# Modulation of a gated two-branch layer computed in three column pieces instead of two

## The chip, the cores and the metric

The kernel runs on one core of a Trainium2 chip. The metric is the device time in microseconds of one execution. Three runs of the kernel before gave 1683.67, 1685.21 and 1689.54 us; the median is 1685.21.

The engines named below: PE (matrix products; PEld is its weight load), DVE (vector), ACT (scalar, activations), POOL (GpSimd) and SP, whose queue issues the DMAs. They run side by side and each executes its instructions strictly in program order, waiting on semaphores for the others.

## The reference

One layer is computed, for 1024 latent tokens and 256 context tokens of 1024 channels, all in fp32. What matters here is its beginning: a modulation vector per stream (latent and context) is a product of a SiLU of the conditioning with `w_ada`; its first 2048 columns are shift and scale for 1024 channels each. The tokens are RMS-normalised, scaled and shifted, and projected by `w_in`.

```python
def rms_norm(t):
    tf = t.astype(jnp.float32)
    return (tf * lax.rsqrt(jnp.mean(tf * tf, axis=-1, keepdims=True) + EPS)).astype(t.dtype)

def modulate(t, shift, scale):
    return rms_norm(t) * (1 + scale) + shift
...
        mod_x = jax.nn.silu(c) @ w_ada[layer] + b_ada[layer]
        mod_c = jax.nn.silu(c_ctx) @ w_ada[layer] + b_ada[layer]
        sh_x, sc_x, g_x = jnp.split(mod_x[:, None, :], 3, axis=-1)
        sh_c, sc_c, g_c = jnp.split(mod_c, 3, axis=-1)
        pl = project(modulate(x, sh_x, sc_x), w_in[layer])
        pc = project(modulate(ctx, sh_c, sc_c), w_in[layer])
```

Behind it come the two branches (gated linear attention, differential attention), their gates and the output projection. They are not touched.

## The kernel before

Tokens come in ten tiles of 128 (0 to 7 latent, 8 and 9 context), channels in eight blocks k of 128. The projection needs each channel block of the modulated tokens with channels on partitions, split into a high and a low fp32r part; one fp32 product then takes three fp32r products (`mm3`, line 340), recorded at line 335.

**How the order is made.** The kernel is written as many generators. A small planner (`Driver`, line 59) runs them against estimated costs and writes PE's, ACT's, DVE's and POOL's instructions in the order in which it would start them. That order is fixed when the kernel is built, and each engine keeps it whatever the data do on the chip. SP's DMAs are placed by the framework's own scheduler; up to eight of them are in flight. Buffers are counted by tag (`acq` and `rel`, lines 316 and 324): `w` has 18 of 128x512, `raw` 3, `l5` 3, `pl` 4, `g5` (token tiles) 6, `tp` (PSUM for transposes) 2.

**The opening** (`prologue`, lines 488 to 661) has these tasks:

- `loads` (515): the weights of the modulation. Its 1024 channels are taken in two halves. For each block k of rows, half 0 loads shift columns and scale columns separately, 128x512 each; among these loads stand the token tiles 0 to 3 (the table `XL`, 663). Then follow the first two weight tiles of the projection (`RAWS`) and the eight loads of half 1, 128x2x512 each. After that the task waits for `ev_wc` (543), which is set when all of half 1 has been split (564), and only then loads the tiles 4 to 9.
- `xnorm` (498): one token tile: ACT squares it with a sum, POOL makes the reciprocal root, DVE scales the tile.
- `conv` (549): splits half 1 of the modulation weights into high (ACT) and low (DVE) parts.
- `ada` (566): the products. Half 0 runs as 16 full fp32 products with two output rows (latent and context): shift into the PSUM tile `gs`, scale into `go`. Half 1 runs as 32 fp32r products of the split weights. The results are copied out of PSUM (`gs` by ACT, `go` by DVE, 590 to 597), transposed by PE into `gt` (4 channels blocks each for shift and scale), and added to the bias by DVE into `shsc`, from which a block's shift and scale are read.
- the main body (647 to 661): for each token half (tiles 0 to 3, 4 to 7, then 8 and 9) and each block k, it waits for `ev_sh[k // 4]`, transposes four token tiles into `tp`, and starts `hblock` (623): ACT applies scale and shift, POOL makes the high part, DVE the low part.

The projection itself starts with three output tiles at once, going through k = 0 to 7: nine products per k. Its weights are split by a stream of their own (`wstream`, 669).

Of the kernel before, what the change touches and what calls it, by code (L numbers as in the profile page):

```python
# [14 lines left out]
ALU = mybir.AluOpType  # L15
# [5 lines left out]
P = 128  # L21
# [207 lines left out]
class Hybrid:  # L229
# [258 lines left out]
    def prologue(self):  # L488
# [5 lines left out]
        def xload(i):  # L494
            xs[i] = self.t("g5", [P, D])
            self.dma(xs[i], a["x"][0, i * P:(i + 1) * P] if i < 8 else a["ctx"][0, (i - 8) * P:(i - 7) * P])

        def xnorm(i):
            yield from self.acq("p")
            sq = self.t("p", [P, D], BF16)  # L500
            ss = self.t("sm", [P, 1])
            yield self.d.when(xs[i])
            self.rel("p", self.act.activation(sq, xs[i], AF.Square, accum_out=ss))
            yield self.d.when(ss)
            self.pool.tensor_scalar(ss, ss, 1.0 / D, EPS, ALU.mult, ALU.add)
            yield self.pool.tensor_tensor(ss, ss, self.nhalf[:, 0:1], ALU.pow)
            self.d.set(ev_x[i], self.dve.tensor_scalar(xs[i], xs[i], ss, None, ALU.mult))

        ev_x = [Event() for _ in range(10)]
        ev_w = {(k, part): Event() for k in range(NK) for part in range(2)}  # L510
        ev_r = [Event() for _ in range(NK)]
        ev_sh = [Event(), Event()]
        shsc = [self.c(f"shsc{x}", [P, 2, 4, 2]) for x in range(2)]

        def loads():

            for part in range(2):
# [24 lines left out]
            d.set(self.ev_wl[1])  # L542
            yield self.ev_wc
            for i in range(4, 10):
                yield from self.acq("g5")
                xload(i)
                self.d.spawn(xnorm(i))

        def conv():
            for k in range(NK):  # L550
                yield ev_r[k]
                tg, raw = ev_r[k].raw
                ev, tw = ev_w[k, 1], ("w", "pl")[k % 2]
# [12 lines left out]
        def ada(part):  # L566


            m = 4 if part else 2
            pa = []  # L570
            for tg in ("gs", "go"):
                yield from self.acq(tg)
                pa.append(self.t(tg, [m, 512]))
            for k in range(NK):
                yield ev_w[k, part]
                for x, w in enumerate(ev_w[k, part].w):
                    if part:
# [4 lines left out]
                    else:  # L582
                        e = self.mm(pa[x], self.col[:, k:k + 9:8], w, k == 0, k == NK - 1)
                        self.rel("w", e)
                        yield AtPE(0)
                if part:
                    self.rel(("w", "pl")[k % 2], e, 4)
                    yield AtPE(0)
            md = []
            for x, tg in enumerate(("gs", "go")):  # L590
# [10 lines left out]
            pt = self.t("gt", [P, 2, 4, m])  # L601
            for x in range(2):
                yield d.whenpe(md[x])
                for y in range(4):
                    e = self.tr(pt[:, x, y], md[x][:, y * P:(y + 1) * P])
                self.rel("p", e)
            yield self.d.when(pt)
            ss = shsc[part]
            for x in range(2):
                o = 24 + 8 * x + 4 * part  # L610
                e = self.dve.scalar_tensor_tensor(ss[:, x], pt[:, x, :, 0:2], float(x), self.col[
                    :, o:o + 4].unsqueeze(2).to_broadcast([P, 4, 2]), ALU.add, ALU.add)
            if part:
# [9 lines left out]
        def hblock(k, half, pt):  # L623
            ctx = half == 2
            n = 256 if ctx else 512
            s = 1 if ctx else 0
            yield from self.acq("p")
            if not ctx:
                yield from self.acq(f"h{half}", 2)
            v = self.t("p", [P, n])  # L630
            hi, lo = (self.hk[:, x * CTX:(x + 1) * CTX] if ctx else self.t(f"h{half}", [P, n], F32R)
                      for x in (2 * k, 2 * k + 1))
            if ctx:
                self.hc[0][k], self.hc[1][k] = hi, lo
# [3 lines left out]
            yield self.d.when(pt, shsc[k // 4])  # L638
# [10 lines left out]
        for half in (0, 1, 2):  # L649
            idx = [8, 9] if half == 2 else [4 * half + j for j in range(4)]  # L650
            for i in idx:
                yield ev_x[i]
            for k in range(NK):
                yield ev_sh[k // 4]
                yield from self.acq("tp")
                pt = self.t("tp", [P, 512])
                for j, i in enumerate(idx):
                    e = self.tr(pt[:, j * P:(j + 1) * P], xs[i][:, k * P:(k + 1) * P])
                self.d.spawn(hblock(k, half, pt), e)
                yield AtPE(0)  # L660
            self.rel("g5", e, len(idx))

    XL = ({1: (0,), 2: (1,), 4: (2,), 6: (3,)}, {})
    RAWS = 2
    CP = ()
    G0, NG = 3, 2
# [1797 lines left out]
```

## Time and profile before

| | |
|---|---|
| times of three runs, us | 1683.67, 1685.21, 1689.54 |
| profiled execution: span from first to last instruction, us | 1685.9 |
| mean granted clock of PE | 0.994 |
| PE, DVE, ACT, POOL busy, us | 1641.8, 1167.5, 788.4, 601.7 |
| DMA traffic of the whole run | 302.84 MB, mean 180 GB/s |
| busy share of the DMA engines, 10 to 20 us | 1.04 |

The profiled execution has no time of its own besides its span; the span is 0.7 us above the median of the runs.

How to read the lines that follow. A row of the timeline has the start and the length in us, the engine, the source line, the operation, the tile written and the tiles read, shapes and a count; in brackets the idle time before it and what ended it. Neighbouring equal instructions are merged into one row. A full fp32 product shows as two records. A row of busy stretches has, after the stretch and its length, the busy us (and count) of PE, PEld, DVE, ACT and POOL, then the granted clock of PE (1.00 is full), the busy share of the DMA engines and the GB/s that they moved. A row of groups has the count, the busy time in us and the mean in ns, then the idle time before the group and what ended it. Buffer numbers are left out of names: `g` is a token tile, `h` a split block, `gs`/`go` shift and scale in PSUM, `l` and `raw` loaded weights.

### The profile page before, as it was taken

The numbers are of one execution on the slowest core, as the hardware profiler recorded it, in microseconds if no ns is written. First come the engines' busy times: TensorE is split into PE (matmuls) and PEld (weight loads), VectorE is DVE, ScalarE is ACT, GpSimd is POOL, SyncE is SP. The second block draws the span as 40 slices with busy tenths as digits, with TensorE's granted clock in tenths as the row PEclk, the third lists the DMA queues.
The fourth block names the chain that finished last, engine by engine and source line by source line (L and its number), as shares of the span: only waits on it lengthen the run. The fifth ranks groups of instructions, "written<-read, shape, count | busy, mean of one in ns | idle before, by whom it ended". The sixth has DMA issues, their size and how long they took to land.

```text
span 1685.9 us, 24403 instructions
## 1 busy us (share of the span) xinstructions
PE 1641.8 (97%) x8389; PEld 1358.3 (81%) x8389; DVE 1167.5 (69%) x2035; ACT 788.4 (47%) x1624; POOL 601.7 (36%) x649
## 2 busy tenths in 40 slices
PE   8999999999999999999999999999999999999999
PEld 3788788888788888888878888888888787887887
DVE  4797853455578697687762988787787887525694
ACT  4666423343334535455442665556666555411231
POOL 1500200000156475465530446555565555700000
PEclk9999999999999999999999999999999999999999
DMA  8557947687683665645375344345368552279422
GB/s 305 167 205 258 325 164 248 226 282 273 200 258 114 197 203 169 207 134 169 117 196 154 85 128 132 104 116 138 113 169 245 167 157 67 98 234 337 151 100 75
DMA packets 255884, 302.84 MB, mean 180 GB/s; under 512 B 21480, under 2 KB 173968, under 8 KB 255760
## 3 DMA queue, kind: packets, MB, share of 16 engines
q1 hardware_dynamic: 255760, 301.29, 56.9%
q8 instruction: 66, 1.08, 0.3%
q14 instruction: 58, 0.48, 0.1%
HBM read 203.71 MB, written 97.52 MB: 179 GB/s over the span
## 4 chain that ended last, share of the span: by engine, by line
PE 43%; DVE 6%; ACT 2%; DMA 2%; POOL 2%; issue 2%; ACTq 0%; DVEq 0%; POOLq 0%; SPq 0%
PE mc L335 10%; PE mm L335 7%; PE mb L335 7%; PE s L335 6%; PE b L335 5%; DVE sm L197 3%; PE b L361 3%; POOL at L197 2%; DVE e L197 2%; PE go L335 1%; ACT e L197 1%; DMA h<-d_bT 1%; PE mz L335 1%; PE gs L335 1%; PE tp L361 1%
## 5 line engine op out<-in xcount | busy, mean ns | idle before, releaser
L335 PE MATMUL mm<-w,h 128*128 128x512 f32 x1260 | 319.3, 402 | 0.6 <-DVE w L197 0.4
L335 PEld LDWEIGHTS mm<-w,h 128*128 128x128 f32 x1260 | 232.0, 189 | 48.0 <-issue 1.0
L197 DVE TENSOR_REDUCE sm<-s 128x1 f32<-128x1024 f32 (+1 forms) x192 | 194.4, 1037 | 49.0 <-PE s L335 47.4
L335 PE MATMUL mb<-h,wt 128*128 128x512 f32 x744 | 204.5, 407 | 2.5 <-ACT ft L197 2.1
L197 ACT ACTIVATE e<-s,sm 128x1280 f32<-128x1280 f32 x128 | 169.9, 1330 | 68.0 <-DVE sm L197 60.3
L197 POOL TENSOR_TENSOR at<-ac,at 128x512 fp32r<-128x512 f32 x128 | 184.7, 1443 | 10.7
L197 POOL TENSOR_SCALAR at<-ac 128x512 fp32r<-128x512 f32 x128 | 100.6, 786 | 236.0 <-ACT ac L197 166.9
L335 PE MATMUL s<-hk,aq 128*128 128x512 f32 (+1 forms) x768 | 178.2, 365 | 3.2 <-ACT e L197 1.1
L335 PEld LDWEIGHTS mb<-h,wt 128*128 128x128 f32 x744 | 131.1, 190 | 25.9 <-ACT ft L197 3.6
L335 PE MATMUL mc<-h,wt 128*128 128x512 f32 x600 | 141.2, 392 | 1.7 <-DMA h<-d_bT 0.8
L335 PE MATMUL mm<-h,w 128*128 128x512 f32 x576 | 139.4, 398 | 2.7 <-ACT p L197 1.1
L335 PEld LDWEIGHTS s<-hk,aq 128*128 128x128 f32 x768 | 122.3, 190 | 23.9 <-ACT e L197 5.1
L335 PEld LDWEIGHTS mc<-h,wt 128*128 128x128 f32 x600 | 111.3, 188 | 26.9 <-DMA h<-d_bT 3.3
L335 PE MATMUL b<-at,vv 128*128 128x256 f32 x960 | 130.6, 285 | 0.5 <-POOL at L197 0.4
L335 PEld LDWEIGHTS mm<-h,w 128*128 128x128 f32 x576 | 108.6, 191 | 27.0 <-DVE h L197 1.4
L335 PEld LDWEIGHTS b<-at,vv 128*128 128x128 f32 x960 | 122.7, 190 | 5.6 <-POOL at L197 1.2
L197 POOL TENSOR_TENSOR sm<-sm,nhalf 128x2 f32<-128x2 f32 (+2 forms) x94 | 106.1, 1129 | 53.6 <-DVE sm L197 48.1
L197 DVE TENSOR_TENSOR w<-raw,w 128x512 fp32r<-128x512 f32 x120 | 92.5, 789 | 31.5 <-ACT w L197 30.3
L197 ACT ACTIVATE ac<-b 128x512 f32<-128x512 f32 x120 | 71.1, 600 | 84.9 <-PE b L361 79.7
L197 DVE SCALAR_TENSOR_TENSOR e<-e,sm,e 128x1280 f32<-128x1280 f32 x64 | 108.7, 1698 | 0.6
L197 ACT ACTIVATE w<-raw 128x512 fp32r<-128x512 f32 x120 | 72.5, 628 | 70.3 <-DVE raw L197 22.8
L361 PE MATMUL b<-ident,e 128*128 128x128 f32 x598 | 92.5, 276 | 12.4 <-DVE at L197 4.3
(283 smaller groups left out, 2832.5 us busy)
## 6 DMA issues: line engine op xcount, KB each, us to landing
raw<-in_w_in SPq DMA_DIRECT2D x63, 512.0 KB, 4.7
g<-d_s SPq DMA_DIRECT2D x32, 640.0 KB, 5.2
aq<-d_qT SPq DMA_DIRECT2D x128, 128.0 KB, 3.4
d_dv<-pl SPq DMA_DIRECT2D x40, 256.0 KB, 2.2
gv<-d_v SPq DMA_DIRECT2D x40, 256.0 KB, 3.2
d_kT<-pl SPq DMA_DIRECT2D x40, 256.0 KB, 3.0
hk<-d_kT SPq DMA_DIRECT2D x32, 320.0 KB, 5.7
vv<-d_dv SPq DMA_DIRECT2D x16, 640.0 KB, 6.2
```

The lines of the kernel that those rows point to most:

```text
L197: self.ins = f(out, *args, **kw).ins
L335: self.ins = self.nc.tensor.matmul(out, lhsT, rhs, start=start, stop=stop, skip_group_check=more).ins
L361: self.nc.tensor.transpose(out, src, self.ident[:n, :n])
```

## The change

The modulation is cut into three pieces of columns: channels 0 to 255, 256 to 511 and 512 to 1023. For each of the first two, shift and scale columns (256 each) are loaded side by side into one 128x512 tile by one DMA of 128x2x256, and one fp32 product per block of rows computes both; they need the PSUM tile `gs` alone, one copy by ACT, and four transposes. The third piece is loaded, split and computed as half 1 was. Token tiles 0 to 3 are loaded after the odd blocks of rows of piece 0. A channel block waits for its own piece (`piece(k)`). The wait of tiles 4 to 9 for `ev_wc` is gone. In the planner the products of a piece are started by the piece before it.

```diff
-        ev_w = {(k, part): Event() for k in range(NK) for part in range(2)}
+        ev_w = {(k, part): Event() for k in range(NK) for part in range(3)}
...
-        ev_sh = [Event(), Event()]
+        ev_sh = [Event() for _ in range(3)]
+        piece = lambda k: min(k // 2, 2)
...
-            for part in range(2):
+            for part in range(3):
                 for k in range(NK):
-                    src = wada[k * P:(k + 1) * P, 0:2048].rearrange("p (s h c) -> p s h c", h=2, c=512)[:, :, part]
+                    o, n = ((0, 256), (256, 256), (512, 512))[part]
+                    src = wada[k * P:(k + 1) * P, 0:2048].rearrange("p (s c) -> p s c", c=1024)[:, :, o:o + n]
                     ev = ev_w[k, part]
-                    if part == 0:
-                        yield from self.acq("w", 2)
-                        ev.w = [self.t("w", [P, 512]) for _ in range(2)]
-                        for s in range(2):
-                            self.dma(ev.w[s], src[:, s])
-                        d.set(ev, d.when(*ev.w))
+                    if part < 2:
+                        yield from self.acq("w")
+                        ev.w = self.t("w", [P, 512])
+                        self.dma(ev.w.rearrange("p (s c) -> p s c", s=2), src)
+                        d.set(ev, d.when(ev.w))
...
-                    for i in self.XL[part].get(k, ()):
+                    if part == 0 and k % 2:
                         yield from self.acq("g5")
-                        xload(i)
-                        self.d.spawn(xnorm(i))
+                        xload(k // 2)
+                        self.d.spawn(xnorm(k // 2))
...
             d.set(self.ev_wl[1])
-            yield self.ev_wc
             for i in range(4, 10):
...
-            m = 4 if part else 2
+            wide = part == 2
+            m = 4 if wide else 2
+            tags = ("gs", "go") if wide else ("gs",)
...
+                else:
+                    e = self.mm(pa[0], self.col[:, k:k + 9:8], ev_w[k, part].w, k == 0, k == NK - 1)
+                    self.rel("w", e)
+                yield AtPE(0)
...
-            if part == 0:
-                d.spawn(ada(1), prio=-1)
+            if not wide:
+                d.spawn(ada(part + 1), prio=-1)
...
-            ss = shsc[part]
+            ss = shsc[1] if wide else shsc[0][:, :, 2 * part:2 * part + 2]
...
-                yield ev_sh[k // 4]
+                yield ev_sh[piece(k)]
```

More of the change, by code (lines that the diff above doesn't have):

```diff
@@ L552, in conv @@
                 tg, raw = ev_r[k].raw
-                ev, tw = ev_w[k, 1], ("w", "pl")[k % 2]
+                ev, tw = ev_w[k, 2], ("w", "pl")[k % 2]
                 yield from self.acq(tw, 4)
@@ L566, in ada @@
         def ada(part):
-            m = 4 if part else 2
+            wide = part == 2
+            m = 4 if wide else 2
+            tags = ("gs", "go") if wide else ("gs",)
             pa = []
-            for tg in ("gs", "go"):
+            for tg in tags:
                 yield from self.acq(tg)
@@ L575, in ada @@
                 yield ev_w[k, part]
-                for x, w in enumerate(ev_w[k, part].w):
-                    if part:
+                if wide:
+                    for x, w in enumerate(ev_w[k, part].w):
                         prods = [(pa[x], self.cs[:, k], w[0]), (pa[x][:2], self.cs[:, k, :2], w[1])][::-1 if k else 1]
@@ L581, in ada @@
                             e = self.mm(o, c, ww, k == 0 and y == 0, k == NK - 1 and y == 1)
[L582 to L586, printed above, removed]
                     self.rel(("w", "pl")[k % 2], e, 4)
-                    yield AtPE(0)
+                else:
+                    e = self.mm(pa[0], self.col[:, k:k + 9:8], ev_w[k, part].w, k == 0, k == NK - 1)
+                    self.rel("w", e)
+                yield AtPE(0)
             md = []
-            for x, tg in enumerate(("gs", "go")):
+            for x, tg in enumerate(tags):
                 yield from self.acq("p")
@@ L597, in ada @@
                 self.rel(tg, e)
-            if part == 0:
-                d.spawn(ada(1), prio=-1)
+            if not wide:
+                d.spawn(ada(part + 1), prio=-1)
             yield from self.acq("gt")
-            pt = self.t("gt", [P, 2, 4, m])
+            pt = self.t("gt", [P, 2, 4 if wide else 2, m])
             for x in range(2):
[L603 to L606, printed above, removed]
+                yield d.whenpe(md[x if wide else 0])
+                for y in range(4 if wide else 2):
+                    c = (4 * (x if not wide else 0) // 2 + y) * P
+                    e = self.tr(pt[:, x, y], md[x if wide else 0][:, c:c + P])
+            self.rel("p", e, len(tags))
             yield self.d.when(pt)
-            ss = shsc[part]
+            ss = shsc[1] if wide else shsc[0][:, :, 2 * part:2 * part + 2]
+            n = 4 if wide else 2
             for x in range(2):
-                o = 24 + 8 * x + 4 * part
+                o = 24 + 8 * x + 2 * part
                 e = self.dve.scalar_tensor_tensor(ss[:, x], pt[:, x, :, 0:2], float(x), self.col[
-                    :, o:o + 4].unsqueeze(2).to_broadcast([P, 4, 2]), ALU.add, ALU.add)
-            if part:
+                    :, o:o + n].unsqueeze(2).to_broadcast([P, n, 2]), ALU.add, ALU.add)
+            if wide:
                 e = self.dve.tensor_tensor(ss, ss, pt[:, :, :, 2:4], ALU.add)
@@ L637, in hblock @@
             sc = shsc[k // 4][:, :, k % 4, s:s + 1]
-            yield self.d.when(pt, shsc[k // 4])
+            yield self.d.when(pt, *[sh for sh in shsc[k // 4:k // 4 + 1]])
             e = self.act.activation(v, pt[:, :n], AF.Identity, bias=sc[:, 0], scale=sc[:, 1])
@@ L661, in prologue @@
             self.rel("g5", e, len(idx))
-    XL = ({1: (0,), 2: (1,), 4: (2,), 6: (3,)}, {})
     RAWS = 2
```

## The prediction

> **What bounds the kernel now.** I read the page's head and engine row first, then the stretches of busy time, then the timeline of the first 65 us, which is all the diff touches.
>
> ```profile
> span 1685.9 us, 24403 instructions
> PE 1641.8 (97%) x8389; PEld 1358.3 (81%) x8389; DVE 1167.5 (69%) x2035; ACT 788.4 (47%) x1624; POOL 601.7 (36%) x649
> 0.00:100.00 100.00, 88.13 (x384) 57.23 (x385) 64.52 (x103) 56.96 (x102) 32.97 (x61) 0.97 0.67 222
> 63.20:80.00 16.80, 16.80 (x98) 14.07 (x99) 12.37 (x19) 13.14 (x28) 10.37 (x16) 1.00 0.21 66
> ```
>
> PE is busy 97% of the span. About 12 of its 44 idle us lie in the first 100 us, and from 63.2 us on it has hardly a gap for some 100 us. What the change does to the whole is therefore the time by which PE comes earlier or later out of the opening. The built orders agree with this: of 8077 PE instructions in the program, the last 7351 stand in the same order in both kernels; POOL's order does not change at all.
>
> Now the opening. PE first runs the sixteen fp32 products of the first modulation half, two records to a product, while the inputs land:
>
> ```profile
> 5.51 1.87 PE L335 MATMUL gs<-w,col 128*2 128x512 f32 x2 [0.29 <-DVE col L197]
> 7.17 1.92 PE L335 MATMUL go<-w,col 128*2 128x512 f32 x2
> ...
> 10.30 1.06 ACT L197 ACTIVATE p<-g 128x1024 bf16<-128x1024 f32 x1 [6.04 <-DMA g<-in_x]
> ...
> 15.33 1.02 PE L335 MATMUL gs<-w,col 128*2 128x512 f32 x2
> 16.19 1.02 PE L335 MATMUL go<-w,col 128*2 128x512 f32 x2
> ...
> 22.45 1.02 PE L335 MATMUL go<-w,col 128*2 128x512 f32 x2
> 23.40 0.41 PE L361 MATMUL gt<-ident,p 2*128 2x2 f32 x4
> 24.71 1.09 PE L361 MATMUL tp<-ident,g 128*128 128x128 f32 x8
> 24.96 1.15 ACT L197 ACTIVATE w<-raw 128x512 fp32r<-128x512 f32 x2 [0.21 <-DMA raw<-in_w_in]
> 28.26 5.49 PE L335 MATMUL mm<-h,w 128*128 128x512 f32 x18
> ```
>
> An fp32 product costs 16.19 - 15.33 = 0.86 us, and at the start 7.17 - 5.51 = 1.66, twice as much. The first product of the projection starts at 28.26. From there to 45.39 PE alternates between 36 projection products and the 32 products of the second half; the next stretch of the projection starts in earnest at 51.61, and after its 36 products PE is held once more:
>
> ```profile
> 36.37 2.88 PE L335 MATMUL mm<-h,w 128*128 128x512 f32 x12
> 39.08 0.63 PE L335 MATMUL gs<-pl,cs 128*2 128x512 f32 x2
> ...
> 44.77 0.62 PE L335 MATMUL go<-pl,cs 128*2 128x512 f32 x2
> ...
> 47.02 1.04 ACT L197 ACTIVATE p<-g 128x1024 bf16<-128x1024 f32 x1
> 47.28 0.17 DVE L197 TENSOR_TENSOR shsc<-shsc,gt 128x16 f32<-128x16 f32 x1
> 48.06 1.43 ACT L197 ACTIVATE p<-tp,shsc 128x512 f32<-128x512 f32 x2
> 51.61 9.60 PE L335 MATMUL mm<-h,w 128*128 128x512 f32 x35 [1.05 <-DVE h L197]
> 61.05 1.03 PE L361 MATMUL tp<-ident,g 128*128 128x128 f32 x8
> 63.15 3.70 PE L335 MATMUL mm<-h,w 128*128 128x512 f32 x15 [1.07 <-ACT p L197]
> ```
>
> **The change, part by part.** *Landing times.* SP issues in order and the DMA engines are full. Before, x tile 0 is the end of 1.573 MB issued and lands for 10.30, and the second projection weight is the end of 7.34 MB and lands for 24.96: 5.77 MB in 14.66 us, 0.393 MB/us. In the changed program SP's order is: piece 0 with tiles 0 to 3 (4.19 MB), two projection weights, two 512 KB loads of piece 2, and only then the eight loads of piece 1. So although piece 0 is smaller (its last weight, at 3.67 MB, lands at 15.6 us, where the first half's came at about 22), piece 1 spans 6.29 to 8.39 MB: its first load lands at 10.30 + (6.55 - 1.573)/0.393 = 23.0 us, its last at 27.7. Its rows are now runs of 1 KB where they were of 2 KB. The nearest rows are a stretch in which all packets are small, and the opening:
>
> ```profile
> DMA packets 3757, 1.89 MB, mean 315 GB/s; under 512 B 64, under 2 KB 3757, under 8 KB 3757
> ...
> DMA packets 1778, 4.01 MB, mean 401 GB/s; under 512 B 196, under 2 KB 196, under 8 KB 1778
> ```
>
> The first has 503 B a packet at 315 GB/s. A 256 KB load in 1 KB runs thus costs between 0.67 us (0.393 MB/us) and 0.83 us; I take 0.75, in the middle. With nine such loads up to piece 1's first and sixteen to its last, these land at 23.7 (23.0 to 24.4) and 29.0 (27.7 to 30.3). The Trainium skill, "DMA: Bandwidth & Descriptors", Specifications, gives 512 B as the smallest run at line rate, by which the runs would cost nothing and the lower ends would hold; the 315 GB/s row does not quite bear that out.
>
> *Piece 1 stands in front of the projection.* PE's built order is now eight products of piece 0, four transposes of the shift and scale, eight of tokens, eight fp32 products of piece 1, and then the first nine projection products. This is a wait that was not there: the operands of those nine are ready by about 24.5 us (tile 3 lands near 17, its scaling and two transposed blocks follow), but PE stands at piece 1, and behind it queue all of the projection and, through its buffers, the split of piece 2. Sixteen fp32 products are executed in both kernels; before, all ran while PE had nothing else to do. Eight of them now start at 23.7 and cost at least 8 x 0.86 = 6.9 us, so they cannot end before 30.6 (29.9 with the early landing). And the clock:
>
> ```profile
> 23.80:27.20 3.40, 1.81 (x16) 1.55 (x16) 3.11 (x7) 3.19 (x6) 0.34 (x1) 1.00 1.06 386
> 27.20:30.60 3.40, 3.40 (x13) 2.67 (x12) 2.58 (x3) 2.91 (x6) 2.72 (x4) 0.50 1.02 375
> 47.70:51.10 3.40, 1.96 (x12) 1.08 (x10) 2.68 (x4) 3.40 (x8) 2.78 (x5) 1.00 0.88 219
> 51.10:54.50 3.40, 2.89 (x7) 2.33 (x8) 3.40 (x5) 0.76 (x2) 1.95 (x2) 0.50 1.05 219
> ```
>
> A stretch of 3.4 us in which PE is busy 1.8 to 2.0 is followed by one at a clock of 0.50. In the changed kernel PE does, between about 16.5 and 23.7, only 12 transposes: 0.41 + 1.09 = 1.5 us in 7. So piece 1 starts at half clock and stays there until the end of a busy stretch; with the boundaries of this execution (23.8, 27.2) for about 3.5 us, in which half the work is done: 1.75 us lost. Piece 1 ends at 23.7 + 6.9 + 1.75 = 32.3. The ends are 29.9 (no slow stretch) and 24.4 + 6.9 + 3.4 = 34.7 (6.8 us of it). The Trainium skill, "TensorE: Matmul & The Clock Gate", part 1, says that the gate's windows run freely and that an idle window halves the clock until a busy one has passed; by it the same program would lose 1.7 to 3.4 us here, changing from run to run. The trace agrees as far as the two 0.50 stretches go.
>
> The projection then starts at 32.3 instead of 28.26: +4.0 (+1.6 to +6.4).
>
> *From there to the last modulation product.* The work is the same 36 and 32 products, plus what has moved behind the start: eight token transposes (channels 256 to 511, 1.09 us) and four of shift and scale (0.41): +1.5. The slow stretch 27.2 to 30.6, which before fell on the first 18 products (33.59 - 28.26 = 5.33 us by the row below, against 18 x (39.08 - 36.37)/12 = 4.07), is already paid: -1.3.
>
> ```profile
> 33.59 0.63 PE L335 MATMUL gs<-w,cs 128*4 128x512 f32 x2
> ```
>
> The split of piece 2 is paced, as before, by PE's releases of its buffers. Between two such groups the new order leaves 2.3 us of PE work or more (six projection and four modulation products at 0.226), against 0.62 + 2 x 0.69 = 2.0 on ACT and DVE:
>
> ```profile
> L197 ACT ACTIVATE pl<-raw 128x512 fp32r<-128x512 f32 x8 | 4.6, 623 | 5.8 <-PE gs L335 5.8
> ...
> L197 DVE TENSOR_TENSOR pl<-raw,pl 128x512 fp32r<-128x512 f32 x8 | 5.2, 686 | 3.4 <-ACT pl L197 3.4
> ...
> L197 ACT ACTIVATE p<-gs 2x512 f32<-2x512 f32 x1 | 0.6, 587 | 0.6 <-PE gs L335 0.6
> ```
>
> I cost it at nothing (1 us if that cover were gone). The copy of piece 1 out of PSUM, now ACT's instead of one by DVE (0.59), lies under the nine products behind it (2.0), and two more small operations for shift and scale lie beside PE; both nothing. The last modulation product ends 4.0 + 1.5 - 1.3 = 4.2 later, at about 49.6.
>
> *The gap at 45 to 51 us.* Before it lasted 51.61 - 45.39 = 6.2 us, partly because the square of tile 5 held ACT from 47.02 until 48.06, 0.6 us after shift and scale were ready at 47.45. Tiles 4 and 5 no longer wait for the split: on all three engines their normalisation now stands ahead of the gap. In its place stand two splits of projection weights, in DVE's order directly ahead of shift and scale. Durations:
>
> ```profile
> L197 POOL TENSOR_SCALAR h<-p 128x512 fp32r<-128x512 f32 x8 | 6.7, 858 | 4.3 <-ACT p L197 4.2
> ...
> L197 DVE TENSOR_TENSOR h<-p,h 128x512 fp32r<-128x512 f32 x8 | 6.9, 885 | 1.1 <-POOL h L197 1.1
> ```
>
> Without the splits shift and scale would be ready 2.1 us after the last product, as before, and one block through ACT (0.72), POOL (0.86) and DVE (0.89) would end the gap 4.6 us after it. The two splits put 2 x 0.69 in front: 6.0. Gain 0.2 (1.6 if they come early, a loss of 1 if late).
>
> *The second gap.* PE's 36 products end at 61.21 and it resumes at 63.15, 1.94 us of which 1.03 are transposes: ACT was still squaring context tiles. Tiles 6 to 9 are loaded as soon as their buffers come free, with less in the queue, so I expect these squares to be over: gain 0.6 (0 to 0.9).
>
> *What follows* starts 4.2 - 0.2 - 0.6 = 3.4 us later. Can a later wait swallow it?
>
> ```profile
> 197.92 2.07 PE L335 MATMUL tp<-gb,ones 128*128 128x512 f32 x2 [2.51 <-DVE gb L197]
> DVE g L197 <- ACT g L197: 14.9, 6, 3.6
> ```
>
> PE waits 2.51 us for DVE at 195 us, so up to 2.5 us can vanish. But DVE itself waits 14.9 us in the preceding stretch for ACT's results, which come from PE's own products and shift with it. I take nothing: +3.4 us on the span of 1685.9. The profiled execution is within 0.7 us of the median shown, 1685.2, so on the runs the forecast is 1688.6.
>
> **The rivals.** *Slower beyond doubt:* the same mechanism at its dear end. Piece 1 ends at 34.7, because the half clock lasts two stretches and small runs load at 315 GB/s, and no later wait gives any back: 6.4 + 1.5 - 1.3 = 6.6, less nothing for the gaps, 1691.8. It decides once piece 1 ends after about 34 us. For it: the 0.50 rows and the 315 GB/s. Against: the boundaries of this execution. *No loss, or a small gain:* piece 1 at full clock ends at 29.9 (+1.6 + 1.5 - 1.3 = +1.8), the first gap shrinks to 4.6 (-1.6), the second vanishes (-0.9), DVE's wait swallows 2.5: -3.2, 1682.0. For it: tiles 4 to 9 do come off the gaps. Against: the idle 7 us before piece 1. *Faster as the wording suggests:* piece 1 is hidden as piece 0 is. Then the projection starts when its operands are ready, 24.5 instead of 28.26: -3.8 + 1.5 - 1.3 - 0.2 - 0.6 = -4.4, 1680.8, or a little less if the gaps shrink too. That needs piece 1's weights by 17 us; SP's order brings the last 10 us later, so nothing in it speaks for this.
>
> **How the numbers follow.** A measurement of this kernel can tell about 0.3%, 5 us, from no change. Forecast, piece 1 ending between 31 and 34: 0.50, a time of +1 to +5. Slower rival 0.32; small gain 0.13; the fast case 0.05. The forecast's upper edge lies near the bound, so I give it 0.07 to slower. Faster 0.07, same 0.54, slower 0.39. The forecast alone spans 1686 to 1690.5; for eight in ten I reach from 1683 to 1693.
>
> **What would show it.** In the changed profile: (1) the first projection product near 32 us, after eight pairs of fp32 products at 23 to 32 whose first are 1.7 us apart; (2) a clock of 0.50 around 24 to 27 and 1.00 at 28 to 34; (3) ACT's square of tile 5 ahead of the gap, and shift and scale of piece 2 near 53 us; (4) the eight transposes of the second token half near 65 us, with the products right behind them. I am wrong if PE reaches its first projection product before 29 us, if piece 1's loads land before the two of piece 2 issued ahead of them, or if the delay at 65 us is not the delay at the end.

## The result, and the profile after

| | kernel before | changed kernel |
|---|---|---|
| median of six runs each, us | 1687.47 (1683.67 to 1689.54) | 1697.01 (1691.79 to 1699.11) |
| ratio | 1 | 1.0053, 95% interval 1.0033 to 1.0072 |
| span of the profiled execution, us | 1685.9 | 1696.1 |

The changed kernel is slower by about 9 us, and its time lies above the forecast (1688.6) and above the range. Of the 8.4 us above the forecast 2.3 are the base: the kernel before has a median of 1687.47 over six runs, and of 1685.21 over the three that the forecast started from. As a ratio the forecast is 1.0020, below both intervals measured. A second series gave 1.0036 (1.0022 to 1.0049); it stands among the experiments. The head of the page of the changed kernel and its engine row:

```profile
span 1696.1 us, 24408 instructions
PE 1644.6 (97%) x8389; PEld 1358.5 (80%) x8389; DVE 1166.7 (69%) x2036; ACT 789.8 (47%) x1625; POOL 605.7 (36%) x649
```

PE was idle for 1685.9 - 1641.8 = 44.1 us before and for 1696.1 - 1644.6 = 51.5 us now: 7.4 of the 10.2 us between the two spans are idle time. The other 2.8 are busy time: the work is the same, so it ran at a lower clock. The next view, stretches of busy time in the changed kernel, says where the idle time is, and shows four of the stretches at half clock (stretch, length, busy us of PE, PEld, DVE, ACT and POOL, clock, DMA share, GB/s):

```profile
0.00:100.00 100.00, 84.40 (x358) 51.67 (x359) 57.87 (x98) 54.85 (x99) 35.74 (x61) 0.95 0.63 213
17.00:20.40 3.40, 1.53 (x9) 0.63 (x7) 1.52 (x4) 2.67 (x5) 0.85 (x3) 0.99 1.05 387
20.40:23.80 3.40, 1.33 (x5) 0.93 (x5) 2.89 (x6) 3.03 (x5) 1.03 (x2) 0.50 1.08 359
23.80:27.20 3.40, 3.23 (x4) 0.47 (x5) 1.72 (x3) 0.82 (x2) 0.90 (x1) 0.50 1.10 350
...
204.70:208.10 3.40, 2.07 (x3) 1.04 (x4) 3.40 (x6) 2.34 (x4) 0.71 (x1) 0.50 0.98 357
208.10:211.50 3.40, 3.40 (x10) 2.66 (x9) 2.50 (x3) 0.00 (x0) 2.98 (x2) 0.50 0.92 316
```

In the first 100 us PE is busy 84.40 us where it was 88.13: 3.7 us more idle. Stretches at half clock follow those in which PE did 1.53 and 1.33 us of work in 3.4, and a pair lies at 204.7 us. To the opening, in PE's timeline of the changed kernel:

```profile
23.97 8.61 PE L335 MATMUL gs<-w,col 128*2 128x512 f32 x16 [1.37 <-DMA w<-in_w_ada]
32.51 2.35 PE L335 MATMUL mm<-h,w 128*128 128x512 f32 x9
...
49.14 0.63 PE L335 MATMUL go<-pl,cs 128*2 128x512 f32 x2
...
54.15 2.71 PE L335 MATMUL mm<-h,w 128*128 128x512 f32 x10
58.11 6.19 PE L335 MATMUL mm<-h,w 128*128 128x512 f32 x26 [1.24 <-DVE h L197]
64.14 1.14 PE L361 MATMUL tp<-ident,g 128*128 128x128 f32 x8
67.37 1.02 PE L335 MATMUL mm<-h,w 128*128 128x512 f32 x3 [2.09 <-ACT p L197]
```

Piece 1's products start at 23.97, take 8.61 us in place of 6.9, the projection starts at 32.51 and the last modulation product ends at 49.77. From there the row of 26 products is held 1.24 us, and the gap before 67.37 is longer than before, not shorter. At 67.37, PE is 4.2 us later than in the kernel before (63.15). But the end is 10.2 later. Most of the rest comes near 200 us, at a job that the diff does not touch, again on PE's timeline of the changed kernel:

```profile
175.77 1.43 PE L335 MATMUL mm<-w,h 128*128 128x512 f32 x5 [1.20 <-DVE w L197]
...
177.62 23.31 PE L335 MATMUL mm<-w,h 128*128 128x512 f32 x102
206.03 2.08 PE L335 MATMUL tp<-gb,ones 128*128 128x512 f32 x2 [5.10 <-DVE gb L197]
```

The two waits were 0.36 and 2.51 us in the kernel before: 3.4 us more idle, which with the 3.7 of the opening makes 7.1 of the 7.4.

PE comes to the gate's product, the row into `tp` from `gb`, at 206.03 - 5.10 = 200.93; before it came at 197.92 - 2.51 = 195.41, with as many products done. So PE is 5.5 us later there, of which 0.8 is the first of the two waits and 4.7 is the opening. Further on the same instructions can be compared: a row of twelve products into `gt` starts at 229.11 before and at 238.20 now, 9.1 us later. The two waits and the half clock behind the second thus add 4.4 us to the 4.7 of the opening; the last 1.1 of the 10.2 come behind 400 us, where no order differs.

This is `job_gate` (line 745), which makes the modulation's gate columns. For each of two halves it loads four weight tiles into the `raw` buffers, which it shares with the projection and the pair weights; DVE adds each into `gb` with two operations; then one fp32 product on PE sums `gb` over its rows:

```
yield from self.acq("raw")
raw = self.t("raw", [P, 2, 512])
self.dma(raw, a["w_ada"][0][kk * 256:(kk + 1) * 256, o:o + 512]...)
yield self.d.when(raw)
...
yield self.d.whenpe(gb)
...
e = self.mm(pm, self.ones, gb[:, n], True, True)
```

PE keeps the planned order, so until `gb` is ready nothing behind this product runs. DVE's timeline of the kernel before, from its last long wait to the last step of `gb`:

```profile
184.05 2.89 DVE L197 TENSOR_TENSOR g<-g,g 128x1280 f32<-128x1280 f32 x2 [3.40 <-ACT g L197]
...
195.16 1.31 DVE L197 SCALAR_TENSOR_TENSOR gb<-raw,col,gb 128x512 f32<-128x512 f32 x1 [0.38 <-DMA raw<-in_w_ada]
...
197.12 0.74 DVE L197 SCALAR_TENSOR_TENSOR gb<-raw,col,gb 128x512 f32<-128x512 f32 x1
```

and of the changed kernel:

```profile
188.82 2.90 DVE L197 TENSOR_TENSOR g<-g,g 128x1280 f32<-128x1280 f32 x2 [2.54 <-ACT g L197]
...
201.28 1.77 DVE L197 TENSOR_TENSOR g<-g 128x640 f32<-128x640 f32 x1
...
203.83 0.74 DVE L197 SCALAR_TENSOR_TENSOR gb<-raw,col,gb 128x512 f32<-128x512 f32 x1
...
205.23 0.75 DVE L197 SCALAR_TENSOR_TENSOR gb<-raw,col,gb 128x512 f32<-128x512 f32 x1
```

DVE restarts on the same operation 4.8 us later, as everything is later by then; but from there to the end of `gb` it takes 17.2 us in place of 13.8, with other operations (of a job named `sums`) standing ahead of the last two steps. SP's rows in the two kernels, before

```profile
177.03 0.68 SPq L300 DMA_DIRECT2D raw<-in_w_ada  x1
...
191.06 0.38 SPq L300 DMA_DIRECT2D raw<-in_w_ada  x1
```

and after:

```profile
186.31 0.37 SPq L300 DMA_DIRECT2D raw<-in_w_ada  x1
...
198.33 0.38 SPq L300 DMA_DIRECT2D raw<-in_w_ada  x1
```

The last two gate loads are issued 9.3 and 7.3 us later, more than the 5.5 us by which PE comes later to the product (200.93 after 195.41). In the built programs the sixth gate load, which stood ahead of the first pair weight, now stands behind it: the planner, working from estimated times that had moved, shared out the three buffers and DVE's order in another way.

### The profile page after: what moved, and what is told of

It reads as the page before. It is cut to its first block, busy times and chain, and to the rows that moved or that the text cites. A ratio compares the mean times of both kernels' runs of the same rounds, so it can differ in the third digit from the quotient of the medians.

```text
span 1696.1 us, 24408 instructions
## 1 busy us (share of the span) xinstructions
PE 1644.6 (97%) x8389; PEld 1358.5 (80%) x8389; DVE 1166.7 (69%) x2036; ACT 789.8 (47%) x1625; POOL 605.7 (36%) x649
## 4 chain that ended last, share of the span: by engine, by line
PE 43%; DVE 5%; DMA 2%; ACT 2%; POOL 2%; issue 2%; ACTq 0%; SPq 0%; DVEq 0%; POOLq 0%
PE mc L335 10%; PE mb L335 7%; PE mm L335 7%; PE s L335 6%; PE b L335 5%; PE b L361 3%; DVE sm L197 3%; POOL at L197 2%; DVE e L197 1%; PE go L335 1%; ACT e L197 1%; DMA h<-d_bT 1%; PE mz L335 1%; PE gs L335 1%; PE tp L361 1%
```

## The experiments

The theory had two parts: the opening costs about 4 us because of piece 1's products; the rest is the changed order near 200 us. All ratios are against the kernel before, with 95% intervals; 0.001 is 1.7 us. Of each kernel one execution was profiled.

**The wait alone.** On the kernel before:

```
             d.set(self.ev_wl[1])
-            yield self.ev_wc
             for i in range(4, 10):
```

> The kernel before, with only the wait for the split taken away: modulation stays in two halves, the pieces are not made. Theory (two parts: about 4 us of the 10 us lost come from piece 1's products standing ahead of the projection, the other 5 to 6 us from the gate weights' loads, which the planner puts behind projection loads in the shared buffers between 160 and 200 us): the opening is as before, first projection product at 28.3 us and last modulation product at 45.4, and the planner's order of the gate loads is the same as in the changed kernel, so PE waits about 5 us for gb instead of 2.5 and the end comes 4 to 6 us later, about 1690 to 1691. Rival A (all of the loss comes from the pieces in the opening and grows on its own): the end within 1 us of the kernel before, about 1686. Rival B (tiles loaded earlier take the loss away): the gap before 51.6 shrinks by 1 to 2 us and stays gained, 1684.

Ratio 1.0031 (1.0020 to 1.0041), median 1691.81 against 1686.81. The size was as expected and the wait for `gb` too, 5.10 us. But the opening was not as in the kernel before. PE's timeline of this kernel, then ACT's:

```profile
44.80 0.62 PE L335 MATMUL gs<-w,cs 128*2 128x512 f32 x2 [1.66 <-DVE w L197]
46.36 0.63 PE L335 MATMUL go<-w,cs 128*2 128x512 f32 x2 [0.94 <-DVE w L197]
...
48.23 1.01 PE L335 MATMUL go<-pl,cs 128*2 128x512 f32 x2 [0.47 <-DVE pl L197]
...
202.70 2.08 PE L335 MATMUL tp<-gb,ones 128*128 128x512 f32 x2 [5.10 <-DVE gb L197]
```

```profile
42.35 1.06 ACT L197 ACTIVATE p<-g 128x1024 bf16<-128x1024 f32 x1 [1.96 <-DMA g<-in_x]
...
43.41 0.61 ACT L197 ACTIVATE w<-l 128x512 fp32r<-128x512 f32 x1
```

The square of tile 4 stands in ACT's order ahead of a split of the modulation weights. It waits 1.96 us for its tile, the split waits behind it, and PE behind the split: the last modulation product ends at 49.24 in place of 45.39. The wait that was taken away had kept tiles out of this place.

**The pieces alone.** The changed kernel with `yield self.ev_wc` put back.

> The changed kernel with the wait for the split put back: three pieces, but tiles 4 to 9 load behind the split as before. Theory: the opening is as in the changed kernel, first projection product at 32.5, last modulation product at 49.8 (+4.2 to +4.4), and the gate loads stand in the changed kernel's order, so gb is waited for about 5 us and the end is 9 to 10 us later than before: 1695 to 1697. Rival A (the wait taken away costs the second part): end only 4 to 5 us later, 1690. Rival B (1 KB runs slow all loads): first product of piece 1 later than 24.5.

Ratio 1.0041 (1.0027 to 1.0055), median 1695.09. The projection starts at 33.43, the last modulation product ends at 50.70, and `gb` is waited for 5.10 us. Both halves of the change, each alone, turn the later order.

**The order of the gate loads, alone.** In the changed kernel the pair weights wait until the sixth gate load is placed:

```
                 self.dma(raw, a["w_ada"][0]...)
+                if n == 1 and kk == 1:
+                    self.d.set(self.ev_g6)
...
             yield ev_load
+            yield self.ev_g6
```

> The changed kernel, with one wait added in the planner: the first load of the pair weights goes behind the sixth gate load, which restores the order of the gate loads of the kernel before. Theory: up to 160 us everything as in the changed kernel (+4.2 to +4.8), then the wait for gb falls from 5.1 to about 2.5 us and the end is 4 to 6 us later than the kernel before, about 1690 to 1692. Rival A (the second part of the loss is contention or the clock, not this order): gb still waited for 5 us or the loss appears elsewhere, 1695 to 1697. Rival C (the gate order is only a consequence): the wait falls but pair weights are late instead and PE waits for them, 1694 or more.

And in the kernel before, the reverse: the sixth gate load waits for the first pair weight.

> The kernel before, with one wait added in the planner: the sixth gate load goes behind the first load of the pair weights, which gives about the order of the gate loads of the changed kernel. Opening untouched. Theory: up to 160 us within 0.3 us of the kernel before, then the wait for gb grows from 2.5 to 5 us or more and the end comes 4 to 6 us later, 1690 to 1692. Rival A (the second part comes from the later opening itself): no more than 1 us later, 1686 to 1687.

Gate first: ratio 1.0036 (1.0022 to 1.0050), median 1693.33. Gate behind: 1.0020 (1.0008 to 1.0032), median 1690.94. The gate's product and the row ahead of it in the one kernel, and in the other:

```profile
176.02 21.95 PE L335 MATMUL mm<-w,h 128*128 128x512 f32 x96
202.15 2.07 PE L335 MATMUL tp<-gb,ones 128*128 128x512 f32 x2 [4.18 <-DVE gb L197]
```

```profile
170.75 29.61 PE L335 MATMUL mm<-w,h 128*128 128x512 f32 x129
203.72 1.12 PE L335 MATMUL tp<-gb,ones 128*128 128x512 f32 x2 [3.36 <-DVE gb L197]
```

Both waits moved the way that the theory says, but by 0.9 us each, not by 2.6. They do not measure the loads' order alone, because the planner moved the product too. The row ahead of it in the kernel before is

```profile
172.78 22.63 PE L335 MATMUL mm<-w,h 128*128 128x512 f32 x99
```

With the gate first this row has 96 products, in place of the 102 of the changed kernel: at 0.227 us each the product is asked for 1.4 us earlier. With the gate behind it has 129 in place of 99, and it is asked for 6.8 us later. Counted from the start of that row, the product starts after 26.1 us with the gate first and after 28.4 in the changed kernel; after 33.0 with the gate behind and 25.1 in the kernel before. So with the loads in the order of before, `gb` is ready 2.3 us earlier, most of the 2.6, though PE waits longer for it than that suggests. What else the planner moved with the loads, DVE's order above all, is in these figures, and the wait for the split stays at 1.19 us. The gate-first ratio cannot be told from the changed kernel's.

**The projection ahead of piece 1.** In the changed kernel:

```
+            if part == 1:
+                yield self.ev_h[0, 0]
+                yield AtPE(d.now + 2.4)
             for k in range(NK):
                 yield ev_w[k, part]
```

> The changed kernel, with piece 1's eight products put behind the first twelve projection products in PE's order; the planner then happens to give the gate weights and the DVE work between 160 and 200 us the order of the kernel before. Theory for the opening: the loss there is the 8.6 us of piece 1's products itself, which now run in a stretch in which PE has no idle time left, so turning the order round gains nothing: projection begins at 25 us, the last modulation product still ends at 49.5 to 51. Rival (the prediction's wording, the loss is that the nine products stand behind piece 1): last modulation product at 46 to 47. Theory for the second part: the wait for gb is back at 2.5 us and DVE's split is waited for 0.4 us instead of 1.2, so the end is 3 to 4 us earlier than the changed kernel: 1692 to 1694; if the second part does not depend on the order, 1696 to 1697.

Ratio 1.0032 (1.0020 to 1.0043), median 1691.69. PE's timeline:

```profile
22.54 5.01 PE L335 MATMUL mm<-h,w 128*128 128x512 f32 x12 [0.95 <-POOL h L197]
27.47 7.03 PE L335 MATMUL gs<-w,col 128*2 128x512 f32 x16
...
200.26 1.81 PE L335 MATMUL tp<-gb,ones 128*128 128x512 f32 x2 [2.51 <-DVE gb L197]
```

The projection starts 10 us earlier than in the changed kernel (2.5 earlier than expected, and at half clock), and the last modulation product still ends at 49.94. Up to there it is not the place of piece 1 that costs, but that its eight products are executed once PE has work enough. Further on the place does tell: PE comes to the gate's product at 200.26 - 2.51 = 197.75, 2.3 us later than in the kernel before, where the opening of the changed kernel cost 4.7 (3.5 in the second execution profiled). That difference arises between 62 and 82 us; its cause was not sought.

Near 200 us the planner gave this kernel the order of the kernel before, and the wait for `gb` is 2.51 us to the hundredth, though PE comes later: it is not the lateness that makes the wait grow. In this profile the stretch from 170 to 211 us adds nothing to the delay. In the six profiles with the changed kernel's order there and the gate's product in its place (the changed kernel twice, its two halves, and the next two runs) it adds 3.2 to 4.7 us; the two waits are 3.4 us of longer idle time in each, and the clock makes the difference.

**Piece 1's loads earlier.** In the changed kernel, the event that lets SP issue the first projection weights is set after piece 1 instead of piece 0.

> The changed kernel with piece 1's eight loads issued directly behind piece 0's and tile 3, ahead of the first two projection weights and of piece 2. Theory: all sixteen fp32 products run while PE has nothing else to do, as in the kernel before, so the projection begins near 28.3 us and the last modulation product ends at 45.4 to 46.5; the order of the work at 160 to 200 us stays that of the changed kernel, so gb is still waited for about 5 us and the end is 4 to 5 us later than before: 1690 to 1692. Rival (the pieces themselves, with 1 KB runs, cost the 4 us): projection at 31 to 33, 1695 to 1697.

Ratio 1.0046 (1.0029 to 1.0064), median 1693.86: a miss for both sides. The projection starts at 28.70 as expected, but the last modulation product ends at 51.50. The rows of ACT and of PE in this kernel:

```profile
44.61 1.06 ACT L197 ACTIVATE p<-g 128x1024 bf16<-128x1024 f32 x1 [1.91 <-DMA g<-in_x]
```

```profile
47.06 1.01 PE L335 MATMUL gs<-w,cs 128*2 128x512 f32 x2 [2.87 <-DVE w L197]
```

It is the wait of the first experiment again: where the projection is early, the freed tiles' squares get in front of the split.

**PE kept busy.** In the changed kernel, nine products without use ahead of tile 3's first transpose and five behind block 1, into a spare PSUM tile:

```
+                self.nc.tensor.matmul(idle, self.col[:, 0:9:8], self.ident, start=True, stop=True)
```

> The changed kernel with 14 small products whose result is not used, in PE's two waits between 19 and 24 us, so that PE is busy there; all other orders are unchanged. Theory: the clock of 0.53 in the stretch 24.0 to 27.4 becomes 1.00, piece 1's products all cost 0.86 us, and the first projection product comes 1.7 us earlier, at 30.8, the last modulation product at 48.1; the end 1 to 2 us earlier than the changed kernel, 1695 to 1696, less than the runs can tell. Rival (piece 1 is bound by its loads): the clock is 1.00 but the first projection product comes no earlier than 32.

Ratio 1.0032 (1.0021 to 1.0043), median 1691.99. PE's timeline and one stretch:

```profile
23.56 7.03 PE L335 MATMUL gs<-w,col 128*2 128x512 f32 x16 [0.75 <-DMA w<-in_w_ada]
30.52 2.34 PE L335 MATMUL mm<-h,w 128*128 128x512 f32 x9
```

```profile
24.00:27.40 3.40, 3.40 (x9) 0.67 (x8) 2.10 (x4) 0.63 (x1) 0.00 (x0) 1.00 1.11 351
```

The clock is 1.00, piece 1 takes 7.0 us, and the projection starts 2.0 us earlier: 1.6 from piece 1's clock, 0.4 because it starts earlier. The clock term of the opening is shown on the trace. The time fell by 3.5 or 0.7 us, against the first or the second series of the changed kernel, which is not clear of noise.

**The gate's product later.** The planner places it 10 us later, 42 places behind in PE's order:

```
-            yield self.d.whenpe(gb)
+            yield AtPE(self.d.whenpe(gb) + 10.0)
```

> The changed kernel, with the gate's product planned 10 us later, so that some 43 more projection products stand ahead of it in PE's order; opening unchanged. Theory: PE's wait of 5.1 us for gb, and the half clock that follows it (2.7 us), go away, and nothing on PE's path needs the gate soon: 5 to 8 us earlier than the changed kernel, 1689 to 1692. Rival A (DVE is behind with everything at that place, so PE waits for its splits or copies instead): the wait moves to another tile, 1695 to 1697. Rival B (the later loss is not this wait): no change.

Ratio 1.0006 (0.9992 to 1.0021), median 1687.88: nearly all of the loss is gone. PE's row:

```profile
207.12 1.02 PE L335 MATMUL tp<-gb,ones 128*128 128x512 f32 x2
```

There is no wait, and no stretch at half clock behind it. But the kernel before has a wait there too, so the same edit was made to it, and to each half of the change:

> The kernel before, with the gate's product planned 10 us later, as in the run of the changed kernel with that edit; from the pair weights on, both then have the same order of loads and products, so their difference is the price of the change's opening alone. Theory (opening costs 4 to 5 us, the rest of the 10 was the wait for gb): the wait of 2.5 us and the half clock behind it go away, 2.5 to 4 us faster than the kernel before, 1682 to 1684, that is 4 to 6 us ahead of the changed kernel with the same edit (1687.9). Rival (the opening costs nothing that lasts, everything was the later order): within 1.5 us of 1687.9.

> The kernel before without the wait for the split, and with the gate's product planned 10 us later. Theory: the 5 us that taking the wait away cost were the wait for gb too (5.1 us against 2.5, and its half clock), apart from 1 to 2 us in the opening, where PE was held 3.1 us between 28 and 49 us and gained most of it back later: 1684 to 1686. Rival (tiles loaded earlier cost the split its place, and that lasts): 1688 or more.

> The changed kernel with the wait for the split put back, and with the gate's product planned 10 us later: the pieces alone, without the wait for gb. Against the kernel before with the gate's edit (ratio 0.9976), the wait alone cost 4 us in the opening, the whole change 5. Theory (the pieces' own cost is the eight fp32 products that PE does after 24 us, about 4 us, and the freed tiles add little to it because PE is late enough for the split): 3 to 5 us behind that kernel, 1686 to 1688, ratio 0.9994 to 1.0006. Rival (all of the opening's loss comes from tiles loaded early): within 1.5 us of it, 1682 to 1684.

| | as it was | gate's product later | worth of the edit, us |
|---|---|---|---|
| kernel before | 1 | 0.9976 (0.9965 to 0.9987) | 4.0 |
| wait taken away | 1.0031 | 1.0000 (0.9989 to 1.0010) | 5.2 |
| pieces alone | 1.0041 | 0.9994 (0.9984 to 1.0004) | 7.9 |
| both: the change | 1.0053, again 1.0036 | 1.0006 (0.9992 to 1.0021) | 7.9, 5.1 |

(Differences of the ratios times 1687 us.) In the second column all four load into the `raw` buffers in the same order from the pair weights on, and PE has no wait over 0.5 us between 120 and 215 us in any of the profiles, so it prices the opening: the wait alone costs 4.0 us, the pieces alone 3.0, both 5.1, each to within about 3 us. Whether the two add can't be told from that; that with the pieces PE comes late enough for the split would be a reason why they need not. In one profile of each, the same PE instruction near 320 us comes 2.0, 3.0 and 2.6 us later than in the kernel before with this edit. The kernel before with this edit is faster than both kernels, by 0.24% (0.13 to 0.35).

The changed kernel itself, once more:

> The changed kernel itself once more, to know its loss against the kernel before to within 2 us. Theory: the opening's 5 us and 4 us for the wait for gb and its half clock add, 1.005 to 1.006. If the ratio is below 1.004, the second part is worth 2 us rather than 4.

Ratio 1.0036 (1.0022 to 1.0049), median 1695.05 against 1688.42, the wait for `gb` 5.11 us. The opening's 5.1 us are then followed by 3.9 us (first series) or 1.1 us (this one), each to within about 4 us, so the medians alone do not show a second part. The profiles do: PE's delay grows between 170 and 211 us by 4.4 us in the first and by 4.7 in this one, and not at all where the order of before came back. The sign, the place and the size are shown by the traces; how much of it lasts to the end is not known closer than the medians tell.

**Both edits.** The changed kernel with the gate's product later and PE kept busy; and the kernel before with the gate's product later and twenty products without use in the waits of its opening.

> The changed kernel with both edits that helped it: the gate's product planned 10 us later, and the 14 unused products that keep PE busy between 19 and 24 us. Theory: the two terms add, since they lie in different places: 1687.9 less the 2 to 5 us that keeping busy gave, 1684 to 1686. Rival (the clock loss only moves to another gap): 1687 to 1688.5.

> The kernel before with the gate's product planned 10 us later and twenty unused products in PE's waits at 25.8, 48.0, 50.6 and 62.1 us, so that no stretch there is idle enough to halve the clock. Theory: the half-clock stretches at 27.2 and 51.1 us of the kernel before (3.4 us in all) go away beside the wait for gb: 1678 to 1682, the fastest version here. Rival (the products themselves delay the transposes and blocks behind them): no better than the gate's edit alone, 1682 to 1684.

The first: 0.9987 (0.9977 to 0.9997), median 1683.48; the gains add within the intervals, and the changed kernel's loss is more than made up. Against the kernel before with the gate's edit (0.9976) it is still 1.9 us behind, which is within the noise. The second: 0.9982 (0.9971 to 0.9993), median 1683.11, no better than the gate's edit alone: a miss. Its profile has no stretch at half clock in the first 200 us, but the median does not show the gain. The profile of the gate's edit alone has only one such stretch there, at 27.0 us and worth up to 1.7 us, which is less than the interval can tell.

## Why the prediction was wrong

*Landing and piece 1: right.* First product forecast at 23.7, measured 23.97; projection at 32.3, measured 32.51; last modulation product at 49.6, measured 49.77. The half clock took 1.7 us of piece 1, as forecast, and with PE kept busy piece 1 took 1.6 less. That the first product came where it did rests in part on luck: the price of a load was taken from the middle between two rows.

*"PE stands at piece 1" as the reason: wrong up to 50 us, with the right size.* With the order turned round, the last modulation product ends at the same time. The term is the 6.9 us of fp32 work moved out of PE's idle time, and its clock. Behind 62 us the turned order is 1 to 2 us cheaper.

*The split costed at nothing: right for this kernel only.* There is no PE wait for it between 32.5 and 49.8. The price given in case that cover were gone, 1 us, was too low: with the wait alone taken away PE stood 3.1 us.

*The first gap: a gain as forecast, larger and for other reasons.* From the last modulation product to the end of the 36 products the changed kernel takes 14.5 us (64.30 - 49.77) in place of 15.8 (61.21 - 45.39), a gain of 1.3 where 0.2 was forecast. It lies inside the range given (a loss of 1 to a gain of 1.6). The blocks came earlier than forecast, and no half clock fell there; in the kernel before one lay from 51.1 to 54.5. A split of a projection weight then held them up; its row on ACT in the changed kernel:

```profile
56.09 0.63 ACT L197 ACTIVATE w<-raw 128x512 fp32r<-128x512 f32 x1 [2.40 <-DMA raw<-in_w_in]
```

*The second gap: wrong sign.* Forecast a gain of 0.6, measured a loss of 1.1 (67.37 - 64.30 = 3.07 after 1.94). ACT's rows of the changed kernel:

```profile
62.69 1.06 ACT L197 ACTIVATE p<-g 128x1024 bf16<-128x1024 f32 x1
...
64.08 1.06 ACT L197 ACTIVATE p<-g 128x1024 bf16<-128x1024 f32 x1 [0.24 <-DMA g<-in_ctx]
...
65.14 1.69 ACT L197 ACTIVATE pl<-p 128x128 fp32r<-128x128 f32 x8
...
66.74 1.54 ACT L197 ACTIVATE p<-mm 128x512 f32<-128x512 f32 x3
```

The context squares were not over: their tiles still wait for buffers of tiles 0 to 3, which the first token half frees. Eight small splits stand behind them too, and the copies that free PE's output tiles come last. A stretch at half clock follows the gap:

```profile
68.20:71.60 3.40, 3.40 (x12) 2.56 (x11) 2.06 (x3) 1.41 (x3) 1.78 (x2) 0.51 0.57 193
```

So the opening was forecast at +3.4. It stands at +4.2 on PE's timeline at 67 us and at +4.7 when PE comes to the wait for the split at 175 us (3.5 in the second execution), and the runs with the gate out of the way put it at 5.1, to within 3.

*The carry to the end: the step that failed.* "But DVE itself waits 14.9 us in the preceding stretch for ACT's results, which come from PE's own products and shift with it. I take nothing". That is right for an unchanged order: with the order of before, a later opening finds the same 2.51 us. But the order was not unchanged. The prediction asked of this wait only whether it could swallow time, not whether it could grow, and took PE's and POOL's orders (alike in the last 7351 instructions, alike throughout) for the whole. SP's, ACT's and DVE's orders differ until about 200 us, and they feed the wait. It grew to 5.10 us, DVE's split is waited for 0.8 us longer, and the half clock behind the gap lasts two stretches (204.7 to 211.5 us above) in place of one in this execution. That one, in the stretches of the kernel before:

```profile
197.90:201.30 3.40, 3.38 (x6) 2.06 (x7) 3.30 (x4) 2.62 (x4) 1.81 (x1) 0.50 0.96 254
```

So the term put at nothing measured 4.4 us on the trace: 3.4 of waits and 1.0 of clock. With the opening at 4.7 that makes 9.1 of the 10.2 us in this execution. It is the last sign of being wrong that the prediction named: the delay at 65 us is not the delay at the end.

What is open: which decision of the planner turns the order. With the gate loads put back, and with what the planner moved along with them, `gb` is ready 2.3 of 2.6 us earlier; DVE's order was not undone by itself, and the longer wait for the split stayed.

## What to carry to other kernels

Where a planner writes the order of all engines, an edit at the start can reorder buffers and queues far behind it: compare every engine's order up to the last difference, and price each wait on the bounding engine there in both directions. Work moved out of idle time has to be paid for where the engine has none: here 6.9 us of it, and 1.7 of clock, made the opening 3.5 to 4.7 us later. So ask first whether the engine is idle, and then what stands in front of what. A product whose result nobody needs soon should not stand where its operands are just ready: placing it some 40 products later was worth 4 to 8 us here.

## What the runs showed of the hardware

An operation of DVE with two tiles from SBUF took longer where POOL ran one beside it. In the changed kernel's timeline of POOL, then of DVE:

```profile
192.66 1.67 POOL L197 TENSOR_TENSOR p<-p,ggla 128x512 f32<-128x512 f32 x1 [9.18 <-DVE p L197]
195.16 1.73 POOL L197 TENSOR_TENSOR p<-p,ggla 128x512 f32<-128x512 f32 x1 [0.82 <-DVE p L197]
```

```profile
195.67 1.78 DVE L197 TENSOR_TENSOR g<-h,h 128x512 f32<-128x512 f32 x1
...
198.23 0.68 DVE L197 TENSOR_TENSOR g<-h,h 128x512 f32<-128x512 f32 x1
```

The same sum takes 0.68 us alone and 1.78 us beside POOL's second product: it ends 0.56 us after that one does. The Trainium skill, "SBUF — State Buffer", Who interferes with whom, says that a VectorE instruction with two inputs from SBUF contends with a GpSimd instruction (POOL here) that reads SBUF. The same page of the Trainium skill, Summary: rules for kernel authors, adds that the second one to issue blocks until the first is done. The rows agree: this meeting costs DVE 1.1 us. By the durations of DVE's rows from its restart to the last step of `gb`, there are three such meetings in the changed kernel, 3.2 us in all, and two in the kernel before, 1.7 us.

The runs of one program also spread by about as much as the change is worth: the changed kernel's six by 7.3 us. Each stretch at half clock costs up to 1.7 us, and the profiled execution of the changed kernel has eight before its last instruction against six in the kernel before, at other places in each execution.
